# Index scores in groups of four, another order of attention units, sparse scaling on ScalarE, and low weights made by an adding transfer

## The chip, the cores and the metric

The kernel runs on one core of one Trainium2 chip. A core has five engines that run their own instruction queues in order and meet at semaphores: TensorE (PE, matrix products), VectorE (DVE), ScalarE (ACT), GpSimd (POOL) and SyncE (SP, which here only issues transfers). PE reads its operands from SBUF and writes to the eight banks of PSUM; DVE and ACT empty the banks. The metric is the device time of one execution in microseconds, as the median of several runs; lower is better.

## The reference, cut to what matters

Three transformer-like blocks follow each other on x, 512 tokens of 1024 features in float32. Block 1 is sparse attention with a gated unit and a convolved feed-forward; block 3 a state space and delta rule mixer. The change lies in block 2, which runs twice (l = 0, 1):

```python
h = rms_norm(x, g_mix[layer]);  proj = h @ w_in[layer]
qa, ka, va, iq, ik, iw, qb, kb, vb = split(proj)          # rope on qa, ka, iq, ik, qb, kb
dots = einsum('bqhd,bsd->bqhs', iq, ik) * IDX_DIM ** -0.5  # 8 index heads of 32
score = einsum('bqhs,bqh->bqs', relu(dots), iw * IDX_HEADS ** -0.5)
_, idx = top_k(where(admissible, score, -inf), 128)
out_a = softmax(qa . ka[idx]) . va[idx]                    # sparse attention, 8 heads of 64
out_b = differential attention of qb, kb, vb               # 4 heads, each the difference of two maps
x = x + concat([out_a, out_b]) @ w_out
x = x + (silu(h2 @ w_gate) * (h2 @ w_up)) @ w_down         # h2 = rms_norm(x, g_ffn)
```

## The kernel before

The stream x is held with features on the partitions, eight tiles of 128 x 512. A product in full precision is made of three passes of PE on operands split in two parts, high and low: high by high, high by low, low by high. The split of weights is made on the chip. `load_piece` (L278 to L285) lets SP fetch a piece of up to 128 x 1024 to a raw buffer (one of four), ACT makes the high part `whi` by a cast (L283), and DVE the low part `wlo` as raw less high (L284). `whi` and `wlo` each go round three buffers (`WS`), so a piece can be split as soon as PE has used up the third one before it. `lin_steps` (passes at L350 to L352) makes a block of 128 output features by 24 passes of 512 columns, and `tok_steps` (L333 to L335) does products with tokens on the partitions.

Block 2 begins with projections of the index queries and keys and their rotary embedding. `rope` copies a result (ACT, L871), lets four small transfers turn its halves (issued by ACT, L874), and forms the result with a product on POOL (L875), one on DVE (L876) and a sum on POOL (L877). After that come the index scores: for the query tiles qt = 1, 2, 3 (256, 384, 512 keys) and eight heads of 32 rows each, three passes into a bank of kind `s` (three banks), then a relu on ACT (L940) and an accumulation with the head's weight on DVE (L941). For each of the three tiles 16 calls of `top8` (L924, L925) find the 128 largest, one maximum of eight and one replacement each; they are queued in `top`, and a last step turns what is left into a mask. Then vB is projected (36 passes a token tile and half), and attention is mixed.

Attention has eight units, pairs of heads: 0 to 3 are differential, 4 to 7 sparse. A step is a unit and one of four query tiles. PLAN is the order of the 32 steps. In step j the scores of step j + 2 are formed (`scores` L354 to L374: six passes `s`, a masked reduction on DVE at L366, an exponential on ACT at L369), then `select` runs queued `top8` calls, then `turned` transposes the weights (L382, copied by ACT at L384), then the values are multiplied. Between them `feed` takes steps of `fill`: projections of the later units' queries and keys (`heads_steps`), of vA (`wtB`) and, when all of a layer's outputs of units 0 to 3 are there, the first half of the output product (`wout`, columns 512 on, in eight half pieces of 128 x 512). Before sparse weights are transposed, DVE scales them with the reciprocal of their row sum (L1027).

The order of instructions on each engine is made by a scheduler from the order of the program, its own costs and the buffers that come free; engines then run their queues in that order. So the diff alone does not tell what stands where in a queue.

Of the kernel before, what the change touches and what calls it, by code (L numbers as in the profile page):

```python
# [12 lines left out]
F32 = mybir.dt.float32  # L13
# [7 lines left out]
P = 128  # L21
# [9 lines left out]
# ---------------------------------------------------------------- host layout  # L31
def kpieces(w):
    """[K, M] -> [M/128, 128, K/128 * 128]: one block of columns per row, the contraction on partitions."""
    k, m = w.shape
    a = w.reshape(k // P, P, m // P, P).transpose(2, 1, 0, 3)
    return np.ascontiguousarray(a).reshape(m // P, P, k)


def kmajor(w):
    """[K, N] -> [128, K/128 * N]."""  # L40
    k, n = w.shape
    return np.ascontiguousarray(w.reshape(k // P, P, n).transpose(1, 0, 2)).reshape(P, -1)


def colvec(v):
    """[n * 128] -> [128, n]."""
    return np.ascontiguousarray(np.asarray(v).reshape(-1, P).T)
# [23 lines left out]
def prep(i):  # L71
# [22 lines left out]
    # block 1  # L94
# [43 lines left out]
    # block 2  # L138
# [31 lines left out]
    # block 3  # L170
# [27 lines left out]
# ---------------------------------------------------------------- device code  # L198
class Build:
    def __init__(self, tc, aps, offs, ctx):  # L200
        self.tc, self.nc, self.aps, self.offs = tc, tc.nc, aps, offs
        self.ctx = ctx
        self.uid = 0
        self.sb = ctx.enter_context(tc.tile_pool(name="sb", bufs=1))
# [15 lines left out]
    def t512(self, dt=F32, name="t"):  # L220
        """A [128, 512] slot, taken in program order and given back with free()."""
# [15 lines left out]
    def set_ring(self, **kinds):  # L237
        """Slots that short-lived tiles of a kind go round; 0 gives them back."""
# [13 lines left out]
    def banks(self, **kinds):  # L252
        """Which PSUM banks each kind of product goes round."""
# [22 lines left out]
    # weights: one DMA of [128, n <= 1024], then the exact two-part split  # L276
    def load_piece(self, ap):
        nc = self.nc  # L278
# [7 lines left out]

    def split(self, src, name="s", tiles=None):
        """src [128, n] F32 (SBUF or PSUM) -> hi, lo."""
# [6 lines left out]
    def lin_T(self, ap, xs, tag="mm", piece=None):  # L295
        """ap [128, K] (one block of 128 output rows); xs: list of (hi, lo) per k-tile -> PSUM [128, 512]."""
        return last_of(self.lin_steps(ap, xs, tag, piece))

    def lin_steps(self, ap, xs, tag="mm", piece=None):
        """lin_T, a k-tile a step; the last step gives the result."""  # L300
# [16 lines left out]
    def tok_steps(self, ap, n, xs, done, wide=1):  # L317
        """ap [128, 8 * n]: tokens on partitions, PSUM [128, n] per token tile to done(tt, ps)."""
# [22 lines left out]
    def scaled(self, o, scale, name):  # L341
        """o * scale in two parts."""
# [4 lines left out]
    def mm3(self, out, w, x, start=True, stop=True):  # L347
        """out (+)= w.T @ x, either operand in two parts."""
# [5 lines left out]
    def scores(self, q, k, qt, masks, mx, sm):  # L354
        """Per half: exp(max - (q.k + mask)) with its row sums; q carries the turned sign."""
# [19 lines left out]
    def turned(self, t, qt):  # L375
        """[queries, keys] -> the blocks of keys on partitions, [128, block, 128 queries]."""
# [10 lines left out]
    def rsqrt(self, y, v, pool=False):  # L387
        """y = v ** -0.5 on small [128, n] tiles; v is SBUF and positive."""
# [17 lines left out]
    def bcast_cols(self, col_of_tt, tag="at"):  # L406
        """[128 tokens, 128 (broadcast)] stationary per token tile -> PSUM [128, 512] rows."""
# [5 lines left out]
    def bcast_pairs(self, cols, tag="at"):  # L413
        """cols [128 tokens, 4, 2] -> PSUM [128 = (2, 64), 512]."""
# [4 lines left out]
    # sums of squares of the residual stream, and what follows from them  # L419
# [19 lines left out]
    def col_sums(self, *accs):  # L439
        """-> PSUM [128 tokens, 4]: sums over the partitions."""  # L440
# [9 lines left out]
    def stat_end(self, st):  # L450
        """-> [128 tokens, 4]: 1 / rms"""
# [13 lines left out]
    def norm_in(self, x, g, hi, lo):  # L465
        """hi + lo = x * g, g a per-partition column."""
# [6 lines left out]
    # ------------------------------------------------------------ block 1  # L473
    def block1(self, x, B, first, g_next, stats):
# [36 lines left out]
        # the overlapping windows of the compressed keys and values, position pairs on partitions  # L511
# [99 lines left out]
        # relative bias strips, sign turned: strip[p, h, c] = -bias[bucket(p + 384 - c)], masked where negative  # L611
# [30 lines left out]
        # the two halves of the spatial gating unit, in parts that go between others  # L642
# [28 lines left out]
        # q / k norms per head  # L671
# [16 lines left out]
        # compressed branch probabilities, transposed to [(r, n), q]  # L688
# [85 lines left out]
        # selected and windowed branches, head pair by head pair: scores ahead of transposes and values, with parts  # L774
        # of projections in between
# [63 lines left out]
        # convolved gated feed-forward, in two halves of its width  # L839
# [26 lines left out]
    # ------------------------------------------------------------ block 2  # L866
    def rope(self, ps, dim, cs, sn):
        """Rotary embedding of PSUM ps with the tables cs, sn."""
# [11 lines left out]
    def block2(self, l, x, xg, st, G, g_next, stats):  # L880
# [38 lines left out]
        # index scores and the 128 largest per query  # L919
# [7 lines left out]
        for qt in range(1, NT):  # L927
# [3 lines left out]
            for h in range(8):  # L931
                hs = slice(32 * (h % 4), 32 * (h % 4) + 32)
                ps = self.pst("s", "is")
                self.mm3(ps[:, :N], [p[hs, qt * P : N] for p in idx[1 + h // 4]], [p[hs, :N] for p in idx[0]])
                w = iw[:, qt, h : h + 1]
                if h == 0:
                    nc.vector.tensor_scalar(sc[:, :N], ps[:, :N], 0.0, w, op0=ALU.max, op1=ALU.mult)
                else:
# [35 lines left out]
        # A unit is a pair of heads (two maps of one, or two that share a block of rows), a step a unit's tile of  # L974
        # queries: scores two steps ahead, then transposes, then values, with parts of projections in between.
# [44 lines left out]
        # sparse attention over the selected keys  # L1020
# [95 lines left out]
        for _ in fill:  # L1116
            pass
# [628 lines left out]
```

## Time and profile before

| what | us |
|---|---|
| runs of the kernel | 3119.2, 3116.98, 3124.82 |
| median | 3119.2 |
| span of the profiled execution, first to last instruction | 3123.8 |
| block 2, layer 0 (index scores to first half of output), about | 711 to 1007 |
| block 2, layer 1 (the same), about | 1404 to 1700 |

Of the profiled execution the span is recorded, and no time of its own beside it; it lies within the range of the three runs. A row of windows gives each engine's busy time in a stretch, the number of instructions in parentheses, then the granted clock of PE as a share of full speed (1.00 is 2.4 GHz and 0.50 is 1.2 GHz), the share of time that DMA engines were busy, and what they moved. A row of a timeline gives start, length, engine, line, operation, what is written and read, shape and how many are drawn together; in brackets stands how long the engine had been idle before it and what released it. Busy time of DVE or ACT counts only where PE waits for it.

### The profile page before, as it was taken

Reading aid. Unit: us, or ns where it says so; the run is one execution under the profiler, and the core shown is the slowest. Engines: PE = TensorE matmul, PEld = TensorE weight load, DVE = VectorE, ACT = ScalarE, POOL = GpSimd, SP = SyncE. Lnnn points to the kernel's source line nnn. Section 1 sums busy time; section 2 is a strip of 40 time slices with the busy share of each in tenths; the row PEclk is TensorE's granted clock in tenths of the full one; section 3 lists DMA queues with packets and bytes.
Section 4 is the critical chain, followed back from the end, with each engine's and each line's share of the span. In section 5 each row is a group of like instructions: output and inputs, shape, how many; then the busy total and the mean of one; then the engine's idle time right before and its main releaser. Section 6 shows DMA issues by size and latency. Waiting matters only on the chain.

```text
span 3123.8 us, 40875 instructions
## 1 busy us (share of the span) xinstructions
PE 3052.9 (98%) x15416; PEld 2437.1 (78%) x15416; DVE 1785.8 (57%) x3400; ACT 1231.4 (39%) x2261; POOL 440.5 (14%) x411
## 2 busy tenths in 40 slices
PE   8999999999999999999999999999999999999998
PEld 6867888887677888887677888877777888888886
DVE  6576655647976333348866333369874665543333
ACT  4365433434455222234454222347543433322222
POOL 0001000011221101121211101110820000211011
PEclk9999999998999999998899999999999999999999
DMA  5402223332212223332213233236434222322322
GB/s 175 125 22 77 90 80 109 99 100 81 74 52 92 95 81 108 97 99 80 72 47 99 93 91 102 79 107 199 155 99 155 85 86 88 108 95 78 110 83 74
DMA packets 124052, 299.95 MB, mean 96 GB/s; under 512 B 28440, under 2 KB 40792, under 8 KB 123856
## 3 DMA queue, kind: packets, MB, share of 16 engines
q1 hardware_dynamic: 115696, 285.79, 29.2%
q10 hardware_dynamic: 7680, 9.97, 1.2%
q8 instruction: 122, 2.00, 0.3%
q0 software_dynamic: 480, 1.57, 0.1%
q14 instruction: 74, 0.61, 0.1%
HBM read 272.52 MB, written 14.79 MB: 92 GB/s over the span
## 4 chain that ended last, share of the span: by engine, by line
PE 87%; DVE 6%; DMA 2%; ACT 2%; POOL 1%; issue 1%; ACTq 1%; SPq 0%; DVEq 0%; POOLq 0%
PE p L350 24%; PE p L351 24%; PE p L352 24%; PE s L362 2%; DMA rope<-rope 2%; PE tr L382 1%; PE ss L444 1%; PE p L333 1%; ACTq L874 1%; DVE isc L925 1%; PE O L1036 1%; PE p L335 1%; PE p L334 1%; POOL rope L877 1%; DVE m L924 1%
## 5 line engine op out<-in xcount | busy, mean ns | idle before, releaser
L350 PE MATMUL p<-xh,whi 128*128 128x512 f32 x2360 | 955.4, 405 | 10.6 <-ACT xh L467 7.2
L283 ACT CAST whi<-wraw 128x1024 fp32r<-128x1024 f32 (+4 forms) x528 | 495.5, 940 | 1181.3 <-PE p L351 851.5
L351 PE MATMUL p<-xl,whi 128*128 128x512 f32 x2360 | 949.4, 402 | 0.5 <-DVE xl L468 0.5
L352 PE MATMUL p<-xh,wlo 128*128 128x512 f32 x2360 | 946.5, 401 | 1.1 <-DMA wraw<-in_b_cw1k 1.1
L284 DVE TENSOR_TENSOR wlo<-wraw,whi 128x1024 fp32r<-128x1024 f32 (+4 forms) x528 | 599.9, 1138 | 325.1 <-ACT whi L283 311.9
L350 PEld LDWEIGHTS p<-xh,whi 128*128 128x128 f32 x2360 | 448.4, 190 | 120.9 <-issue 8.8
L352 PEld LDWEIGHTS p<-xh,wlo 128*128 128x128 f32 x2360 | 447.5, 190 | 107.5 <-issue 4.8
L351 PEld LDWEIGHTS p<-xl,whi 128*128 128x128 f32 x2360 | 448.2, 190 | 103.1 <-issue 5.0
L350 PE MATMUL p<-acth,whi 128*128 128x512 f32 x704 | 277.8, 395 | 0.0
L352 PE MATMUL p<-acth,wlo 128*128 128x512 f32 x704 | 277.7, 394 | 0.0
L351 PE MATMUL p<-actl,whi 128*128 128x512 f32 x704 | 277.5, 394 | 0.0
L1612 POOL TENSOR_TENSOR g<-g,rbc 128x512 f32<-128x512 f32 x66 | 114.0, 1728 | 808.5 <-ACT g L1611 808.5
L436 POOL TENSOR_TENSOR sqacc<-sqacc,sq 128x512 f32<-128x512 f32 x63 | 97.4, 1550 | 777.0 <-ACT sq L434 776.8
L1614 DVE TENSOR_TENSOR g<-g,p 128x512 f32<-128x512 f32 x66 | 45.4, 688 | 238.7 <-PE p L352 238.7
L352 PEld LDWEIGHTS p<-acth,wlo 128*128 128x128 f32 x704 | 132.2, 188 | 31.6
L351 PEld LDWEIGHTS p<-actl,whi 128*128 128x128 f32 x704 | 132.2, 188 | 31.5
L350 PEld LDWEIGHTS p<-acth,whi 128*128 128x128 f32 x704 | 132.2, 188 | 31.3
L1610 DVE TENSOR_TENSOR g<-p,rbc 128x512 f32<-128x512 f32 x66 | 45.7, 692 | 188.1 <-PE p L352 188.1
L369 ACT ACTIVATE stile<-stile,sm 128x128 f32<-128x128 f32 (+3 forms) x192 | 106.8, 557 | 83.3 <-DVE sm L366 72.1
L1634 DVE TENSOR_TENSOR x<-x,p 128x512 f32<-128x512 f32 x96 | 66.0, 688 | 108.1 <-PE p L352 107.9
L333 PE MATMUL p<-whi,xh 128*128 128x256 f32 (+2 forms) x352 | 104.6, 298 | 0.3 <-ACT rope L871 0.3
L334 PE MATMUL p<-wlo,xh 128*128 128x256 f32 (+2 forms) x352 | 102.9, 293 | 0.0
(457 smaller groups left out, 4183.4 us busy)
## 6 DMA issues: line engine op xcount, KB each, us to landing
wraw<-in_b_wup SPq DMA_DIRECT2D x176, 512.0 KB, 3.3
wraw<-in_b_win SPq DMA_DIRECT2D x118, 512.0 KB, 3.6
wraw<-in_b_wdn SPq DMA_DIRECT2D x64, 512.0 KB, 3.5
wraw<-in_b_wout SPq DMA_DIRECT2D x48, 256.0 KB, 2.7
wraw<-in_b_wdn SPq DMA_DIRECT2D x64, 192.0 KB, 2.3
rope<-rope ACTq DMA_DIRECT2D x128, 64.0 KB, 2.3
row<-rows SPq DMA_DIRECT2D x32, 256.0 KB, 4.4
wraw<-in_b_wtC SPq DMA_DIRECT2D x8, 512.0 KB, 4.0
```

Source lines behind the costliest of these rows:

```text
L283: nc.scalar.copy(hi, raw)
L284: nc.vector.tensor_tensor(lo, raw, hi.bitcast(F32), op=ALU.subtract)
L333: mm(ps, xs[k][0][:, ts], wh[:, s], start=k == 0, stop=False)
L334: mm(ps, xs[k][0][:, ts], wl[:, s], start=False, stop=False)
L350: mm(out, w[0], x[0], start=start, stop=False)
L351: mm(out, w[0], x[1], start=False, stop=False)
L352: mm(out, w[1], x[0], start=False, stop=stop)
L362: self.nc.tensor.matmul(out[g][:, :n], q[i][hs, qt * P : n], k[j][hs, :n], start=c == 0, stop=c == 2)
L369: nc.scalar.activation(t[:, :n], t[:, :n], AF.Exp, bias=mx[:, g : g + 1], scale=-1.0, accum_out=sm[:, g : g + 1])
L436: eng.tensor_tensor(accs[i], accs[i], sq, op=ALU.add)
L1612: nc.gpsimd.tensor_tensor(g, g, rbc, op=ALU.mult)
L1634: nc.vector.tensor_tensor(x[m], x[m], ps, op=ALU.add)
```

## The change

Four edits, all in block 2. First, index scores are formed for four heads at a time: of each of the three passes the four heads (on the four quarters of PE's rows) follow each other, and the kind `s` has four banks (2 to 5) instead of three, `mm` three instead of four, in this stage. Second, PLAN places all steps of units 0 to 3 ahead of those of unit 4, and `select` runs three calls a step in place of four. Third, the scaling of sparse weights moves from DVE to ACT. Fourth, from the first step of mixing to the end of the first half of the output product, pieces of weights are split by `load_piece_rmw`: ACT makes high by a copy and low = -high by a second one, and POOL issues a transfer that reads the same weights from memory and adds them to low. These are 24 pieces a layer: 14 of heads, 2 of `wtB`, 8 half pieces of `wout`.

```diff
+    def load_piece_rmw(self, ap):
+        nc = self.nc
+        n = ap.shape[1]
+        raw = self.t([P, 1024], tag="wraw", bufs=self.WR, name="wraw")[:, :n]
+        nc.sync.dma_start(raw, ap)
+        hi, lo = (self.t([P, 1024], tag=tg, bufs=self.WS, dt=F32R, name=tg)[:, :n] for tg in ("whi", "wlo"))
+        nc.scalar.copy(hi, raw)
+        nc.scalar.activation(lo, hi.bitcast(F32), AF.Copy, scale=-1.0)
+        nc.gpsimd.dma_start(lo, ap, accum_op=ALU.add)
+        return hi, lo
...
+        self.banks(mm=(0, 1, 6), s=(2, 3, 4, 5), at=(7,))
+        quarter = [slice(32 * r, 32 * r + 32) for r in range(4)]
...
-            for h in range(8):
-                hs = slice(32 * (h % 4), 32 * (h % 4) + 32)
-                ps = self.pst("s", "is")
-                self.mm3(ps[:, :N], [p[hs, qt * P : N] for p in idx[1 + h // 4]], [p[hs, :N] for p in idx[0]])
+            for hg in range(2):
+                pss = [self.pst("s", "is") for _ in range(4)]
+                for c, (i, j) in enumerate(((0, 0), (0, 1), (1, 0))):
+                    for ps, hs in zip(pss, quarter):
+                        nc.tensor.matmul(
+                            ps[:, :N], idx[1 + hg][i][hs, qt * P : N], idx[0][j][hs, :N], start=c == 0, stop=c == 2
+                        )
...
-                nc.vector.tensor_scalar(tb[g][:, :N], tb[g][:, :N], f[:, g : g + 1], None, op0=ALU.mult)
+                nc.scalar.activation(tb[g][:, :N], tb[g][:, :N], AF.Copy, scale=f[:, g : g + 1])
...
         fill = filling()
         fed = [0]
+        self.rmw = True
...
-            select(4 * (j + 1))
+            select(3 * (j + 1))
...
         for _ in fill:
             pass
+        self.rmw = False
...
-PLAN = "00 01 02 03 10 11 12 13 20 40 21 22 41 42 23 30 31 32 33 43 50 51 52 53 60 61 62 63 70 71 72 73"
+PLAN = "00 01 02 03 10 11 12 13 20 21 22 23 30 31 32 33 40 41 42 43 50 51 52 53 60 61 62 63 70 71 72 73"
```

In the queues this gives the following, for layer 0. On PE, the first three heads of the last query tile's index scores (`is`, one number a head; `idxh` and `idxl` are the parts of index queries and keys) before:

```order
L350 MATMUL is_6587<-idxh_6151,idxh_6200 128x512
L351 MATMUL is_6587<-idxl_6152,idxh_6200 128x512
L352 MATMUL is_6587<-idxh_6151,idxl_6201 128x512
L350 MATMUL is_6592<-idxh_6151,idxh_6200 128x512
L351 MATMUL is_6592<-idxl_6152,idxh_6200 128x512
L352 MATMUL is_6592<-idxh_6151,idxl_6201 128x512
L350 MATMUL is_6599<-idxh_6151,idxh_6200 128x512
L351 MATMUL is_6599<-idxl_6152,idxh_6200 128x512
L352 MATMUL is_6599<-idxh_6151,idxl_6201 128x512
```

and after, where the lines have moved with the text:

```order
L952 MATMUL is_6587<-idxh_6151,idxh_6200 128x512
L952 MATMUL is_6587<-idxl_6152,idxh_6200 128x512
L952 MATMUL is_6588<-idxh_6151,idxh_6200 128x512
L952 MATMUL is_6588<-idxl_6152,idxh_6200 128x512
L952 MATMUL is_6589<-idxh_6151,idxh_6200 128x512
L952 MATMUL is_6589<-idxl_6152,idxh_6200 128x512
L952 MATMUL is_6587<-idxh_6151,idxl_6201 128x512
L952 MATMUL is_6588<-idxh_6151,idxl_6201 128x512
L952 MATMUL is_6589<-idxh_6151,idxl_6201 128x512
```

The passes of a head no longer stand next to each other; the heads alternate, by threes at this place, and the fourth follows alone. Of the tile before this one, the first head of each group of four has moved up among the passes of vB: the first stood behind 36 of these and stands behind 2, the fifth behind 15, the other six behind 27 and more.

On DVE, what precedes the first reduction of attention scores (`stile` from `s`) in layer 0, before (`isc` are the index scores of a tile, `m` the eight largest):

```order
L924 MAX m_1528_7194<-isc_6474 128x8
L925 MATCH_REPLACE isc_6474<-m_1528_7194,isc_6474 128x256
L924 MAX m_1529_7197<-isc_6474 128x8
L925 MATCH_REPLACE isc_6474<-m_1529_7197,isc_6474 128x256
L924 MAX m_1530_7200<-isc_6474 128x8
L924 MAX m_1553_7292<-isc_6530 128x8
L925 MATCH_REPLACE isc_6474<-m_1530_7200,isc_6474 128x256
L925 MATCH_REPLACE isc_6530<-m_1553_7292,isc_6530 128x384
L284 TENSOR_TENSOR wlo_7019<-wraw_7016,whi_7018 128x1024
L1084 TENSOR_SCALAR isc_6474<-isc_6474 128x256
L366 ISA stile_6903,sm_6892<-s_6895,b_cmask_6060 128x128
L366 ISA sm_6892 128x1
```

and after:

```order
L942 MATCH_REPLACE isc_6474<-m_1565_7344,isc_6474 128x256
L942 MATCH_REPLACE isc_6530<-m_1566_7348,isc_6530 128x384
L1106 TENSOR_SCALAR isc_6474<-isc_6474 128x256
L941 MAX m_1587_7417<-isc_6530 128x8
L942 MATCH_REPLACE isc_6530<-m_1587_7417,isc_6530 128x384
L941 MAX m_1588_7420<-isc_6530 128x8
L942 MATCH_REPLACE isc_6530<-m_1588_7420,isc_6530 128x384
L941 MAX m_1589_7423<-isc_6530 128x8
L381 ISA stile_6903,sm_6892<-s_6895,b_cmask_6060 128x128
L381 ISA sm_6892 128x1
L381 ISA stile_6906,sm_6892<-s_6896,b_cmask_6060 128x128
L381 ISA sm_6892 128x1
```

The splits `wlo` are gone from this place, and more of the second tile's search stands ahead of the first reduction.

On POOL, the stretch before that holds the rope operations of the later units:

```order
L875 TENSOR_TENSOR rope_8092<-rope_8092,tab_6100 128x512
L877 TENSOR_TENSOR rope_8092<-rope_8092,rope_8093 128x512
L875 TENSOR_TENSOR rope_8454<-rope_8454,tab_6100 128x512
L877 TENSOR_TENSOR rope_8454<-rope_8454,rope_8455 128x512
L875 TENSOR_TENSOR rope_8540<-rope_8540,tab_6100 128x512
L877 TENSOR_TENSOR rope_8540<-rope_8540,rope_8541 128x512
L875 TENSOR_TENSOR rope_8657<-rope_8657,tab_6100 128x512
L877 TENSOR_TENSOR rope_8657<-rope_8657,rope_8658 128x512
L875 TENSOR_TENSOR rope_8770<-rope_8770,tab_6100 128x512
L877 TENSOR_TENSOR rope_8770<-rope_8770,rope_8771 128x512
```

and after, from the same unit on, with the issues of the adding transfers for vA, heads and the first half pieces of the output between them:

```order
L890 TENSOR_TENSOR rope_7869<-rope_7869,tab_6100 128x512
L892 TENSOR_TENSOR rope_7869<-rope_7869,rope_7870 128x512
L890 TENSOR_TENSOR rope_7966<-rope_7966,tab_6100 128x512
L892 TENSOR_TENSOR rope_7966<-rope_7966,rope_7967 128x512
L299 DMA wlo_8108<-in_b_wtB 128x1024
L299 DMA wlo_8127<-in_b_wtB 128x1024
L890 TENSOR_TENSOR rope_8090<-rope_8090,tab_6100 128x512
L892 TENSOR_TENSOR rope_8090<-rope_8090,rope_8091 128x512
L299 DMA wlo_8362<-in_b_win 128x1024
L299 DMA wlo_8488<-in_b_win 128x1024
L299 DMA wlo_8591<-in_b_win 128x1024
L890 TENSOR_TENSOR rope_8467<-rope_8467,tab_6100 128x512
```

Each `DMA` row is an issue that POOL makes when ACT has written the negated high part; what follows it in the queue comes after it.

## Rows read from the trace of the kernel before

**Rows 1.** The page: busy time, share of the span, instructions of each engine.
```profile
PE 3052.9 (98%) x15416; PEld 2437.1 (78%) x15416; DVE 1785.8 (57%) x3400; ACT 1231.4 (39%) x2261; POOL 440.5 (14%) x411
```

**Rows 2.** Windows of busy time in us; the last is of layer 1.
```profile
711.00:740.00 29.00, 24.80 (x129) 19.14 (x124) 18.03 (x21) 12.77 (x25) 9.87 (x7) 0.83 0.38 112
740.00:772.00 32.00, 30.04 (x194) 26.29 (x193) 27.41 (x73) 14.43 (x25) 0.29 (x2) 0.78 0.12 37
772.00:845.00 73.00, 66.26 (x310) 50.17 (x310) 68.67 (x189) 31.66 (x86) 20.14 (x21) 0.92 0.30 91
845.00:975.00 130.00, 126.92 (x760) 93.09 (x758) 90.71 (x255) 70.10 (x184) 23.60 (x23) 1.00 0.17 50
1465.00:1538.00 73.00, 65.80 (x309) 49.93 (x310) 69.95 (x191) 31.67 (x86) 20.88 (x22) 0.91 0.31 90
```

**Rows 3.** Waits of PE, 740 to 980: total us, times, longest.
```profile
PE s L362 <- ACT kh L291: 6.6, 4, 2.9
...
PE s L362 <- DVE sm L366: 1.7, 1, 1.7
```

**Rows 4.** Waits of PE in layer 1, 1434 to 1669.
```profile
PE s L362 <- ACT kh L291: 8.6, 4, 3.3
```

**Rows 5.** Timeline of PE, index scores: start, length, instruction, [idle before].
```profile
745.02 0.82 PE L350 MATMUL is<-idxh,idxh 32*128 32x512 f32 x3
745.61 0.65 PE L351 MATMUL is<-idxl,idxh 32*128 32x512 f32 x3
746.04 0.65 PE L352 MATMUL is<-idxh,idxl 32*128 32x512 f32 x3
747.35 1.28 PE L350 MATMUL is<-idxh,idxh 32*128 32x512 f32 x2 [0.66 <-ACT relu L940]
```

**Rows 6.** Groups by form, 733 to 751: count, busy us, mean ns, idle.
```profile
L941 DVE SCALAR_TENSOR_TENSOR isc<-relu,iw,isc 128x512 f32<-128x512 f32 x6 | 4.4, 741 | 0.8 <-ACT relu L940 0.8
...
L940 ACT ACTIVATE relu<-is 128x512 f32<-128x512 f32 x7 | 3.9, 597 | 3.6 <-PE is L352 3.6
```

**Rows 7.** Timeline of all engines, the rope chain of one k.
```profile
791.78 2.44 ACTq L874 DMA_DIRECT2D rope<-rope  x4
...
796.66 1.28 POOL L875 TENSOR_TENSOR rope<-rope,tab 128x512 f32<-128x512 f32 x1 [6.05 <-DMA rope<-rope]
...
798.65 2.11 POOL L877 TENSOR_TENSOR rope<-rope,rope 128x512 f32<-128x512 f32 x1 [0.71 <-DVE rope L876]
...
800.80 0.62 ACT L291 CAST kh<-rope 128x512 fp32r<-128x512 f32 x1 [3.12 <-POOL rope L877]
...
801.47 0.49 PE L362 MATMUL s<-kh,qh 64*128 64x128 f32 x3 [2.13 <-ACT kh L291]
```

**Rows 8.** Window of the ten microseconds around that wait.
```profile
800.00:810.00 10.00, 8.53 (x31) 5.91 (x31) 8.30 (x29) 3.81 (x14) 3.83 (x6) 0.66 0.24 74
```

**Rows 9.** Groups by form, 757 to 850.
```profile
L284 DVE TENSOR_TENSOR wlo<-wraw,whi 128x1024 fp32r<-128x1024 f32 x11 | 13.9, 1274 | 0.0
...
L283 ACT CAST whi<-wraw 128x1024 fp32r<-128x1024 f32 x12 | 12.5, 1044 | 7.0 <-PE p L351 6.1 <-PE p L335 0.9
...
L924 DVE MAX8 m<-isc 128x8 f32<-128x384 f32 x16 | 8.9, 556 | 0.2
L925 DVE MATCH_REPLACE8 isc<-m,isc 128x384 f32<-128x384 f32 x16 | 8.7, 543 | 0.0
```

**Rows 10.** Line L1027, both layers: ns min/median/max, first and last start.
```profile
L1027 DVE TENSOR_SCALAR stile<-stile,sm x64: 275/413/1418, 845.7 to 1657.8; 128x128 f32<-128x128 f32 x16, 128x256 f32<-128x256 f32 x16, 128x384 f32<-128x384 f32 x16, 128x512 f32<-128x512 f32 x16
```

**Rows 11.** DMA issues, 686 to 1007: count, KB each, us to landing.
```profile
wraw<-in_b_win SPq DMA_DIRECT2D x15, 512.0 KB, 3.8
...
wraw<-in_b_wout SPq DMA_DIRECT2D x16, 256.0 KB, 2.7
```

**Rows 12.** DMA issues by POOL in block 3, 2190 to 2262.
```profile
sys<-dAT POOLq DMA_DIRECT2D x2, 256.0 KB, 6.4
dT<-sys POOLq DMA_DIRECT2D x2, 256.0 KB, 3.7
```

More of the change, by code (lines that the diff above doesn't have):

```diff
@@ L277, in load_piece @@
     def load_piece(self, ap):
+        if self.rmw:
+            return self.load_piece_rmw(ap)
         nc = self.nc
@@ L930, in block2 @@
             msl.append(sc)
-            for h in range(8):
-                hs = slice(32 * (h % 4), 32 * (h % 4) + 32)
-                ps = self.pst("s", "is")
-                self.mm3(ps[:, :N], [p[hs, qt * P : N] for p in idx[1 + h // 4]], [p[hs, :N] for p in idx[0]])
[L935 to L938, printed above, removed]
+            for hg in range(2):
[5 more added lines that the diff above has]
+                        )
+                for h, ps in enumerate(pss, 4 * hg):
+                    w = iw[:, qt, h : h + 1]
+                    if h == 0:
+                        nc.vector.tensor_scalar(sc[:, :N], ps[:, :N], 0.0, w, op0=ALU.max, op1=ALU.mult)
+                        continue
                     r = self.tmp(name="relu")
@@ L1117, in block2 @@
             pass
+        self.rmw = False
         self.free(vA, msl, cmask, mix[4:])
```

## The prediction

> **What bounds the kernel now.** I read the page first. TensorE (PE) is busy for 98% of the span and no other engine for more than 57% [rows 1], so time can be gained only where PE stands still or runs at the lower of its two clock levels (1.2 GHz, 0.5 in the clock column; 2.4 GHz is 1.00). I then cut layer 0 of block 2 into stages by windows of busy time [rows 2]. What a stage lost is its length less PE's busy time weighted with the clock: 29 - 24.80 x 0.83 = 8.4 us in 711 to 740 (index projections, first index scores), 32 - 30.04 x 0.78 = 8.6 us in 740 to 772 (last index scores, projection of vB, first attention scores), 73 - 66.26 x 0.92 = 12.0 us in 772 to 845 (mixing of units 0 to 4 with the search for the 128 largest), and 130 - 126.92 = 3.1 us in 845 to 975. The same stage of layer 1 shows 73 - 65.80 x 0.91 = 13.1 us. That is about 32 us a layer: 64 us, 2%, is the ceiling for everything that the change can give. Even the part it can touch does not all belong to it.
>
> The waits say which engine PE stood waiting for in 740 to 980 [rows 3]: k's high part, which ACT makes, 6.6 us in four waits, against 1.7 us for DVE's score reduction. In layer 1 the wait for k is 8.6 us [rows 4]. DVE is 94% busy in 772 to 845 (68.67 of 73) and ACT 43% [rows 2], so DVE is crowded there, and yet PE's waits name it once. It stands behind the others: in the chain up to the wait at 801.47 [rows 7] the rope DMAs are issued at 791.78, POOL begins its product at 796.66, its sum at 798.65, and ACT's cast at 800.80 releases PE after 2.13 us idle. Of the ten microseconds, the DMAs have almost five and POOL's two products 3.4; DVE stands between them with one operation (from 797.94, where POOL's product ends, to 798.65: 0.7 us). The clock then falls: 0.66 in 800 to 810 [rows 8], which costs 10 - 8.53 x 0.66 = 4.4 us where the idle was 2.1. A wait of about 2 us therefore costs about twice itself.
>
> **Index scores by fours.** A matmul pass 512 wide takes 0.43 us at the lower level (745.61 to 746.04), so 0.215 at the higher. Nine matmuls of three heads that begin at 745.02 have all run when PE falls idle 0.66 us before 747.35, at 746.69 [rows 5]: 1.67 us where nine one behind another would take 9 x 0.43 = 3.9. So heads on different quarters of the rows already run beside each other; the new order does not create that. The row after them says what PE waits for: ACT's relu, so the emptying of banks. The Trainium skill, "TensorEngine Tiling (Array Packing)", section "Theoretical Speedup", gives up to four times for a contraction of 32 tiled by rows; by that, the 27.6 thousand columns of a layer's scores, 11.6 us one behind another, would fall to 2.9 and the change would gain 8 us a layer. By the rows here most of that is had already.
>
> That emptying is DVE's and ACT's: one relu 512 wide takes 597 ns on ACT and one accumulation 741 ns on DVE [rows 6], and neither changes in count. What changes is that four banks instead of three take scores, and that the first heads of the next-to-last tile move up among the passes of vB (the first stood behind 36 of these and now stands behind 2, the fifth behind 15; the other six behind 27 and more), so that 14 heads in place of 16 are left to be emptied in one run, at about 0.74 us each. The losses to be had are the 8.4 and 8.6 us of the first two stages; the last scores still end on DVE's chain. Two heads less and a bank more are 3 x 0.74 = 2.2 us, and the lower clock that such a wait brings, half as much again: I take 3.5 us a layer, between -2 (mm has one bank fewer) and 9 (the stage's whole loss).
>
> **Differential heads first, 3 selections a step.** DVE's search for one tile is spread over more steps: 16 passes at 3 a step instead of 4. A maximum over 384 columns costs 556 ns and its replacement 543 [rows 9], so one selection less per step frees 1.1 us of DVE in a step of about 6 us (32 steps between 772 and 975). The first unit's DVE wait (1.7 us) and some of the fall of the clock behind it can go, but by the order DVE does three and a half passes of the second tile ahead of the first scores, where it had done one pass and two splits (one is in the rows shown, the other 20 rows ahead): 2.5 x 1.1 us more against 2 x 1.27 less, so nothing at that very place. Bounds -2 to 4 us a layer; I take 1.5.
>
> **Sparse scaling on ScalarE.** 32 scalings a layer of 413 ns leave DVE [rows 10], 13 us, and arrive on ACT at about the relu's 597 ns for 512 wide, so about 14 us in all. ACT has 60 us free in 845 to 975 (70.10 of 130) and PE lost 3.1 us there: worth between -2 and 1 us, I take 0.
>
> **Low weights made by a transfer that adds.** 24 pieces a layer: 14 of 512 KB for heads, 2 for vA, 8 of 256 KB for the output. DVE loses 16 x 1.27 + 8 x 0.6 = 25 us a layer [rows 9]; in 757 to 850 that is 13.9 of its 93 us, in which it was nearly full. ACT gets a negated copy for each, priced by the cast beside it at 1.04 us [rows 9]: 16 x 1.04 + 8 x 0.52 = 21 us, of which 12 us fall in 757 to 850, where ACT has room. DVE's relief shortens every chain that passes it (rope, score reduction): of the 12.0 us lost in 772 to 845 I give it a third, 4 us, between 0 and 9; the greater part of the rope chain is DMA and POOL and stays.
>
> The price is a longer way to the low part. Now it is cast and subtraction, 1.04 + 1.27 = 2.3 us [rows 9]. After, it is cast, negated copy, an issue on POOL and a transfer, which must also come after whatever stands ahead of it in POOL's queue. No transfer that adds is in this trace. From the rows [rows 11, 12]: a plain 512 KB from SyncE lands in 3.8 us, 256 KB in 2.7; POOL's own 256 KB land in 3.7 to 6.4. So the low end is 3.8 us for 512 KB and 2.7 for 256, and the high end is twice POOL's worst for 512 KB, 12.8, and 6.4 for 256. I take 5.5 and 4, near POOL's lower rows (its 6.4 was measured in a busy stretch). The way is then 1.04 + 1.04 + 0.6 + 5.5 = 8.2 us for a whole piece and 0.52 + 0.52 + 0.6 + 4 = 5.6 us for a half (0.6 us for the issue is an estimate from ACT's four rope issues in 2.44 us [rows 7]).
>
> What covers it: the ring has three low buffers, so a piece may start when the third before it is used up, with two pieces of PE's work ahead of it. A whole piece is 24 passes x 0.215 = 5.2 us, two are 10.3 us, and attention lies between them: 8.2 is covered. The two vA pieces are used in one tile of tokens together, with only 12 short passes between them, and POOL puts a rope pair ahead of them; I count 2 us of waiting. A half piece is 12 passes, 2.6 us; two are 5.2 us against 5.6: 0.4 us for most of the first halves, where little attention lies between, plus POOL's rope in the queue (1.3 us): 2 us. One of the two waits brings the lower clock, 3 us. Together -7 us a layer. At the low end this is -1, at the high end each of 14 pieces comes (15.5 - 10.3) = 5 us late, less what attention covers, some -30 us a layer.
>
> The Trainium skill, "SBUF — State Buffer", section "SBUF: two separate sides", warns that a transfer issued by POOL starves for descriptors while DVE runs an operation in its two-port mode, such as a float32 copy; this speaks against the change, and by it the first rival below would come true wherever DVE is in that mode. Whether the landings of 3.7 to 6.4 us [rows 12] hold such a delay the rows do not tell.
>
> **Sum.** 3.5 + 1.5 + 0 + 4 - 7 = 2 us a layer, and 2 us a layer for the clock that one wait taken away gives back (half of 4.4, as at 801): 4 us, for two layers 8 us. The profiled execution has a span of 3123.8 us, 4.6 over the median of the runs, 3119.2, and inside their spread (3117.0 to 3124.8); nothing that lies around it is touched, so I take the difference from the median: 3111 us. A measurement of this kernel can tell about 0.3%, 9.4 us, from no change, so the forecast lies at that bound.
>
> **Rivals.**
> - The adding transfer is late everywhere. If the landing is over 8 us for 512 KB, the way (1.04 + 1.04 + 0.6 + 8) passes 10.3 us and PE waits for the low part at about half of the pieces; 5 waits of 2 us a layer, doubled by the clock as at 801, are 20 us against gains of 11: +9 a layer, 3119 + 18 = 3137 us, the time I give this case; with 8 waits 3119 + 42 = 3161. For it speaks that POOL's rows for half the size reach 6.4 us and that POOL's queue also holds the rope chain's two links, which a waiting issue blocks. Against it, that DMA engines are only 17 to 31% busy here [rows 2]. From three late pieces a layer on (12 us against 11) it decides the sign. Chance 0.27.
> - Nothing to be had: PE's waits are the rope chain's (DMA and POOL), DVE and ACT were covered. Then gains of 5 us at the index scores and losses of 5 a layer leave 3119 us. For it, rows 3 and 7. Chance 0.22.
> - The crowded DVE was behind nearly all of it. Then 9 of the 12.0 and 13.1 us in the mixing stage and 8 of the first two come back, with 2 us of waiting: 15 a layer, 3119 - 30 = 3089 us. For it, DVE's 94%; against it, one DVE wait in rows 3. Chance 0.21.
> - My own case, 3103 to 3117 us: 0.30.
>
> Faster by over 0.3% (below 3109.8) takes the third case, half of mine and a little of the second and first: 0.21 + 0.15 + 0.06 = 0.42. Slower (above 3128.6) takes most of the first and a little of the second: 0.28. Within 0.3%: 0.30. The range leaves out the ends of the first and third: 3082 to 3146. My own case spans 3103 to 3117.
>
> **What would show it.** Right: the rows of 740 to 772 show a clock above 0.85; DVE below 85% in 772 to 845; waits of PE for k at most as long as before; waits named "wlo" or the adding transfer only at vA and the first output halves, below 5 us a layer. Wrong: landings of the adding transfer above 8 us, or POOL standing on it while rope is queued; or unchanged waits for k with DVE half empty, which says that DVE never mattered.

## The result, and the profile after

The changed kernel takes 3156.2 us (median of 4 runs, 3150.4 to 3160.4) against 3120.6 for the kernel before (4 runs): ratio 1.0100, interval 1.0081 to 1.0119. It is slower by 1%, outside the range forecast and on the side that the first rival had. The profiled execution took 3157.2 us with a span of 3155.4, 31.6 over the span before.

The page: busy time, the granted clock in 40 slices, and the queue of POOL's transfers.

```profile
PE 3063.4 (97%) x15416; PEld 2444.9 (77%) x15416; DVE 1720.0 (55%) x3288; ACT 1295.7 (41%) x2373; POOL 476.1 (15%) x459
...
PEclk8999999998899999998899999999999999999999
...
q0 software_dynamic: 7392, 22.55, 4.0%
```

DVE lost 66 us of work against [rows 1] and ACT gained 64; POOL's queue moves 22.6 MB. PE's busy time grew by 10.5 us for the same work, which is time at the lower clock, and it stood idle 21 us longer. The same stages as in [rows 2] (length, then PE, PEld, DVE, ACT, POOL busy, clock, DMA share, GB/s; the last is layer 1, shifted by as much as layer 0 had lost):

```profile
711.00:740.00 29.00, 25.10 (x137) 19.36 (x136) 18.32 (x25) 13.07 (x26) 8.51 (x6) 0.88 0.39 115
740.00:772.00 32.00, 28.26 (x196) 25.30 (x195) 29.14 (x79) 16.31 (x26) 3.69 (x5) 0.84 0.24 70
772.00:845.00 73.00, 66.45 (x277) 48.53 (x277) 59.69 (x178) 35.62 (x92) 21.57 (x27) 0.81 0.49 112
845.00:975.00 130.00, 117.61 (x698) 87.58 (x697) 60.96 (x191) 85.50 (x210) 36.89 (x37) 0.99 0.42 97
1480.00:1553.00 73.00, 67.86 (x289) 49.41 (x289) 62.28 (x186) 36.88 (x95) 21.27 (x29) 0.84 0.50 114
```

Counted as in the forecast, length less PE's busy time by the clock, the four stages of layer 0 lose 29 - 25.10 x 0.88 = 6.9, 32 - 28.26 x 0.84 = 8.3, 73 - 66.45 x 0.81 = 19.2 and 130 - 117.61 x 0.99 = 13.6 us, together 48.0, where before they lost 32.1. That is 16 us a layer, and twice that is the difference of the spans. All of it is in the mixing of attention (7.2 and 10.5 us more); the two stages ahead gave back 1.8 us. The row of layer 1 loses 73 - 67.86 x 0.84 = 16.0 us against 13.1. DVE fell to 82% in 772 to 845 as forecast, and PE lost more.

PE's waits in layer 0, 680 to 1020 (total us, times, longest):

```profile
PE s L377 <- ACT kh L306: 6.9, 5, 2.5
PE p L349 <- DMA wlo<-in_b_wtB: 2.9, 2, 1.8
PE p L367 <- DMA wlo<-in_b_wout: 2.5, 2, 1.3
PE is L952 <- ACT vA L927: 2.5, 1, 2.5
PE s L377 <- DVE sm L381: 2.2, 1, 2.2
PE is L952 <- ACT relu L961: 2.1, 1, 2.1
PE O L1017 <- ACT pts L399: 2.0, 2, 1.1
PE p L367 <- DMA wlo<-in_b_win: 1.6, 1, 1.6
```

Seven us are waits for the adding transfer itself (2.9 + 2.5 + 1.6). The wait for k is 6.9 us over this stretch against 6.6 in [rows 3], though DVE has been relieved. The transfers (count, KB, us from issue to landing), to be held against [rows 11, 12]:

```profile
wraw<-in_b_win SPq DMA_DIRECT2D x15, 512.0 KB, 3.8
wlo<-in_b_win POOLq DMA_DIRECT2D x14, 512.0 KB, 5.4
...
wlo<-in_b_wout POOLq DMA_DIRECT2D x8, 256.0 KB, 4.9
...
wlo<-in_b_wtB POOLq DMA_DIRECT2D x2, 512.0 KB, 5.5
```

And one half piece of the output in the timeline (start, length, instruction, idle before it):

```profile
948.31 0.60 ACT L384 ACTIVATE stile<-stile,sm 128x384 f32<-128x384 f32 x1
...
949.05 0.63 ACT L298 ACTIVATE wlo<-whi 128x512 fp32r<-128x512 f32 x1
...
949.98 0.88 POOL L299 DMA_DIRECT2D wlo<-in_b_wout  x1 [3.49 <-ACT wlo L298]
...
954.12 0.50 PE L367 MATMUL p<-oh,wlo 128*128 128x512 f32 x1 [1.31 <-DMA wlo<-in_b_wout]
```

ACT's exponentials stand ahead of the negated copy, POOL has idled 3.49 us for it, issues at 949.98, and PE, 1.31 us idle, gets the low part at 954.12. The way of the low part begins in ACT's queue, and 5.1 us from copy to use are what the prediction had counted without that queue.

### The profile page after: what moved, and what is told of

Read it like the earlier page. It is cut to its first block, busy times and chain, and to the rows that moved or that the text cites. A ratio compares the mean times of both kernels' runs of the same rounds, so it can differ in the third digit from the quotient of the medians.

```text
span 3155.4 us, 40937 instructions
## 1 busy us (share of the span) xinstructions
PE 3063.4 (97%) x15416; PEld 2444.9 (77%) x15416; DVE 1720.0 (55%) x3288; ACT 1295.7 (41%) x2373; POOL 476.1 (15%) x459
## 4 chain that ended last, share of the span: by engine, by line
PE 83%; DVE 6%; DMA 3%; ACT 3%; issue 2%; POOL 1%; ACTq 1%; SPq 0%; DVEq 0%; POOLq 0%
PE p L365 23%; PE p L367 23%; PE p L366 23%; PE s L377 2%; DMA rope<-rope 2%; PE tr L397 1%; PE ss L459 1%; DVE isc L942 1%; PE p L348 1%; PE p L350 1%; PE p L349 1%; ACTq L889 1%; DVE m L941 1%; PE O L1057 1%; PE O L822 1%
## 5 line engine op out<-in xcount | busy, mean ns | idle before, releaser
L286 ACT CAST whi<-wraw 128x1024 fp32r<-128x1024 f32 (+3 forms) x480 | 452.4, 943 | 1159.4 <-PE p L366 825.4
L287 DVE TENSOR_TENSOR wlo<-wraw,whi 128x1024 fp32r<-128x1024 f32 (+3 forms) x480 | 542.8, 1131 | 314.4 <-ACT whi L286 304.5
L365 PEld LDWEIGHTS p<-acth,whi 128*128 128x128 f32 x704 | 132.2, 188 | 31.6
L384 ACT ACTIVATE stile<-stile,sm 128x128 f32<-128x128 f32 (+1 forms) x192 | 106.3, 555 | 51.9 <-DVE sm L381 45.7
```

Of the source, the lines that this page charges most:

```text
L286: nc.scalar.copy(hi, raw)
L287: nc.vector.tensor_tensor(lo, raw, hi.bitcast(F32), op=ALU.subtract)
L365: mm(out, w[0], x[0], start=start, stop=False)
L384: nc.scalar.activation(t[:, :n], t[:, :n], AF.Exp, bias=mx[:, g : g + 1], scale=-1.0, accum_out=sm[:, g : g + 1])
```

## Experiments

All times are medians; a ratio is to runs of the kernel before on the same chip. Where nothing else is said the edit is made to the changed kernel.

**The four edits apart.** Without the adding transfer (`e1_no_add`):

```diff
-        self.rmw = True
```

> The changed kernel with DVE's split kept for all pieces (no adding transfer); the other three edits stay. Theory A (the adding transfer costs the time: PE's waits for the low part, POOL's queue, ACT's second copy): all of the 36 us and a little more come back, 3105 to 3122 us. Theory B (the new order of the steps and 3 selections costs it, because what hid the work of sparse steps is used up earlier): 3140 to 3156 us. Theory C (index scores by fours cost it): 3140 to 3156 us too; the next runs tell B from C.

Measured 3124.2 us, ratio 1.0006 (0.9994 to 1.0017): 2 us above theory A's range, but level with the kernel before, which took 3124.3 us beside it. The kernel before with the adding transfer alone (`e2_add_only`):

```diff
+        self.rmw = True   # and load_piece_rmw
```

> The kernel before with the adding transfer alone (order of steps, 4 selections, index scores and DVE's scaling as before). Theory A: 3145 to 3165 us, with waits of PE for the low part of 5 to 8 us a layer and DVE under 85% busy in the mixing stage. Theories B and C: 3105 to 3125 us.

Measured 3157.1 us, ratio 1.0101 (1.0081 to 1.0120). Each way round, the adding transfer is the whole of the loss: theory A, and the other three edits together are worth nothing that can be told.

Of what theory A expected of `e2_add_only`, though, only the time came. PE waits for the low part 2.4 us in layer 0 and 4.8 in layer 1, not 5 to 8, and DVE is busy 67.22 of the 73 us in 772 to 845, 92% and not under 85%. The waits for k fell, to 3.4 us in layer 0 and 3.9 in layer 1 from 6.6 and 8.6 [rows 3, 4]. What grew is PE's busy time, by 27.4 us against [rows 1], of the 36.2 us by which the span is longer. Its page, two windows, and its waits for k and the low part in 680 to 1020:

```profile
PE 3080.3 (97%) x15416; PEld 2453.8 (78%) x15416; DVE 1737.6 (55%) x3352; ACT 1270.0 (40%) x2309; POOL 477.1 (15%) x459
```

```profile
845.00:975.00 130.00, 123.66 (x663) 89.46 (x662) 61.65 (x209) 72.42 (x182) 36.20 (x37) 0.87 0.41 89
850.00:870.00 20.00, 20.00 (x55) 11.80 (x55) 9.11 (x33) 9.59 (x27) 3.70 (x5) 0.53 0.29 69
```

```profile
PE s L377 <- ACT kh L306: 3.4, 3, 1.7
...
PE p L349 <- DMA wlo<-in_b_wtB: 2.2, 2, 2.0
...
PE p L367 <- DMA wlo<-in_b_win: 0.2, 1, 0.2
```

In 845 to 975 the clock is 0.87 where it was 1.00 before. Ahead of 850 PE had idled 1.08 us for k's high part and 0.79 us for its low part; then it was busy for all of 850 to 870, at 0.53. So a loss of the same size is here mostly time at the lower clock, at this place behind short waits for other things than the low part, and PE's waits for the low part do not measure it. Why the clock falls more often than before is not shown.

The kernel before with the order of steps alone (`e3_plan_only`):

```diff
-            select(4 * (j + 1))
+            select(3 * (j + 1))   # and the new PLAN
```

> The kernel before with the order of steps of the changed kernel and 3 selections a step alone. Theory A: 3112 to 3124 us (my term for this was a gain of 1.5 us a layer). Theory B: 3140 to 3156 us.

Measured 3122.4 us, ratio 0.9994 (0.9981 to 1.0007): nothing. The kernel before with the fours alone (`e4_fours_only`):

```diff
-                self.mm3(ps[:, :N], ...)   # head by head
+                for c, (i, j) in enumerate(((0, 0), (0, 1), (1, 0))):   # four heads a pass, four banks
```

> The kernel before with index scores by fours and their banks alone. Theory A: 3110 to 3120 us (my term for this was a gain of 3.5 us a layer). Theory C: 3140 to 3156 us.

Measured 3134.8 us, ratio 1.0029 (1.0009 to 1.0049), between the theories, with runs from 3114 to 3140. Its profiled execution has lost 1 us up to the start of layer 1's mixing at 1445; in layer 1's mixing, which the edit does not touch, the clock was lower, by these windows:

```profile
1540.00:1600.00 60.00, 58.41 (x328) 44.28 (x328) 46.34 (x136) 32.40 (x93) 11.88 (x15) 0.87 0.13 39
1600.00:1660.00 60.00, 57.74 (x316) 40.71 (x316) 33.37 (x94) 27.64 (x70) 11.29 (x8) 0.91 0.17 51
```

In the kernel before the same two windows show 0.98 and 1.00. Whether the edit causes that is open. The order and the scaling on ACT without fours and without the transfer (`g3_plan_and_scale`):

```diff
-                nc.vector.tensor_scalar(tb[g][:, :N], ...)
+                nc.scalar.activation(tb[g][:, :N], tb[g][:, :N], AF.Copy, scale=f[:, g : g + 1])   # beside the new PLAN
```

> The kernel before with the order of steps, 3 selections and the scaling on ACT, without the fours and without the adding transfer. The fours alone cost 0.3%, the order alone nothing; if these add up: 3112 to 3122 us, the best of all so far. If the scaling loads ACT where it matters: 3125 to 3135 us.

Measured 3122.2 us, ratio 0.9996 (0.9984 to 1.0008). Within its interval it is the kernel before; no version here beats that.

**What in the adding transfer costs.** ACT's copies without any transfer (`h2_copy_then_split`), where DVE overwrites the copy with its split:

```diff
-        nc.gpsimd.dma_start(lo, ap, accum_op=ALU.add)
+        nc.vector.tensor_tensor(lo, raw, hi.bitcast(F32), op=ALU.subtract)
```

> The changed kernel with ACT's negated copy into the low part, which DVE then overwrites with its split; no transfer by POOL, and all slots: ACT's load alone, without the dead buffer. If the copies on ACT cost 16 us: 3135 to 3146 us. If the run with the dead buffer was slow for its order or slots: 3120 to 3130 us.

Measured 3136.9 us, ratio 1.0047 (1.0034 to 1.0059), clear of e1. Busy time in 757 to 1010 of e1 and of this run (columns as in [rows 2]):

```profile
757.00:1010.00 253.00, 241.19 (x1338) 183.04 (x1337) 182.29 (x484) 139.15 (x339) 50.86 (x50) 0.95 0.24 73
```

```profile
757.00:1010.00 253.00, 239.95 (x1280) 178.85 (x1279) 178.66 (x467) 153.00 (x355) 51.89 (x50) 0.95 0.22 70
```

ACT's load goes from 55% to 60%. The two profiled executions took 3132.7 and 3133.1 us, so these windows show the load and not the loss, which stands in the ratios. PE's waits in the same stretch of e1, then of this run:

```profile
PE s L377 <- ACT kh L306: 4.9, 3, 4.0
...
PE O L1017 <- ACT pts L399: 0.3, 1, 0.3
```

```profile
PE s L377 <- ACT kh L306: 6.1, 3, 2.4
...
PE O L1057 <- ACT pts L399: 1.4, 1, 1.4
PE O L1017 <- ACT pts L399: 1.1, 3, 0.5
```

The waits for what ACT makes, k and the transposed weights, rise from 5.2 to 8.6 us, while those for DVE fall. DVE's split also comes after ACT's copy here, which may cost something of its own; the copies into a buffer of their own, below, do not have that. A plain transfer in place of the adding one (`f1_plain_transfer`; the low part then holds the raw weight):

```diff
-        nc.gpsimd.dma_start(lo, ap, accum_op=ALU.add)
+        nc.gpsimd.dma_start(lo, ap)
```

> The changed kernel, where POOL's transfer of the 48 pieces does not add but only writes (the low part then holds the raw weight, so the output is not the reference's); the copies on ACT and all queues stay. Theory A1 (adding itself is slow: the transfer reads both sides): landings fall from 5.4 us to under 4.2 and the time to 3125 to 3138 us. Theory A2 (the way over ACT, POOL's queue and a transfer is too long whatever the transfer does): landings of 4.5 to 5.4 us, 3145 to 3158 us.

Measured 3142.2 us, ratio 1.0061 (1.0047 to 1.0075). Its landings:

```profile
wlo<-in_b_win POOLq DMA_DIRECT2D x14, 512.0 KB, 4.1
...
wlo<-in_b_wout POOLq DMA_DIRECT2D x8, 256.0 KB, 3.4
...
wlo<-in_b_wtB POOLq DMA_DIRECT2D x2, 512.0 KB, 3.9
```

A plain transfer of POOL lands 1.3 to 1.6 us sooner than the adding one. The time lies a little above theory A1's and clear of the changed kernel's: adding itself costs some 0.4% of the 1.0%. PE's waits for the low part are 3.3 us in 757 to 1010 (1.9 + 0.9 + 0.5) against 7.0. Against h2, which has the copies and no transfer, the interval overlaps: with a plain transfer the way over POOL costs nothing that can be told beyond the copies. The adding transfer for heads alone (`f2_heads_only`):

```diff
-        self.rmw = True   # for all fill pieces
+                self.rmw = True   # around the load of a head's piece only
```

> The changed kernel with the adding transfer for the 28 pieces of heads alone; the 4 pieces of vA and the 16 half pieces of the output are split by DVE again. Theory A3 (PE's waits at vA and at the first output halves are most of the loss, as the prediction's term of 7 us a layer had it): 3124 to 3136 us. Theory A4 (the loss lies in the mixing of the heads, by ACT's second copies and POOL's queue in the chain of k): 3140 to 3156 us.

Measured 3142.9 us, ratio 1.0060 (1.0046 to 1.0075). The 4 pieces of vA and the 16 halves make about 0.4% of the 1.0%, the 28 pieces of heads the rest over e1. The time lies in A4's range, but A3's places have a part of the loss too.

**Runs with a dead buffer.** These let PE read DVE's split and do the rest of the work for nothing, into a buffer that nobody reads. To make room for it the pool has two slots (tiles of 128 x 512) fewer. Their control (`g1_two_slots_fewer`), the copies (`f3_copy_only`), and copies and transfers (`f4_unwaited`):

```diff
-NS = 66
+NS = 64
```

> The changed kernel with DVE's split for all pieces and two slots of the pool fewer, nothing else: the control for the two runs with a dead buffer. If ACT's second copy was what cost in those: 3118 to 3128 us, as without the adding transfer. If the missing slots did: 3138 to 3150 us.

```diff
+        nc.scalar.activation(dead, hi.bitcast(F32), AF.Copy, scale=-1.0)
```

> The changed kernel with DVE's split for all pieces, no adding transfer, and ACT's negated copy of 48 pieces written to a dead buffer (two slots fewer to make room): ACT has the work of the change, and PE waits for nothing new. Theory A4, ACT's part: 3138 to 3156 us. If ACT has room: 3118 to 3130 us.

```diff
+        nc.scalar.activation(dead, hi.bitcast(F32), AF.Copy, scale=-1.0)
+        nc.gpsimd.dma_start(dead, ap, accum_op=ALU.add)
```

> As the run before, and POOL also issues the adding transfers, into the dead buffer: all of the change's work on ACT, POOL and the DMA queues is done, but PE reads the low part that DVE makes and waits for none of it. If PE's wait for the low part is the cause: 3118 to 3132 us. If POOL's queue and the DMA traffic are (rope's links stand behind issues): 3140 to 3160 us, with more waiting for k.

Measured 3129.2 us (1.0015, 1.0003 to 1.0028), 3145.2 (1.0073, 1.0060 to 1.0085) and 3152.5 (1.0091, 1.0075 to 1.0106). The copies cost 0.6% over the control, a little more than in the run without the buffer (0.4%). PE's waits for what ACT makes in 757 to 1010, of the control, then of the copies:

```profile
PE s L377 <- ACT kh L306: 4.8, 3, 4.0
...
PE O L1017 <- ACT pts L399: 0.4, 1, 0.4
```

```profile
PE s L378 <- ACT kh L307: 7.0, 4, 2.4
PE O L1058 <- ACT pts L400: 3.5, 2, 1.9
PE O L1018 <- ACT pts L400: 2.1, 1, 2.1
```

They rise from 5.2 to 12.6 us, with the clock at 0.95 in both. f4's interval touches f3's and the changed kernel's, so the transfers beside the copies and PE's wait for the low part are not parted here. Nor is f4 clean: it has one dead buffer, and ACT's next copy into it stood 8 times, 15.2 us over both layers, for the landing of the transfer before. In f4 the 64 KB rope transfers land later than in e1; in the changed kernel, which is as slow, they do not. e1's first, then f4's, then the changed kernel's:

```profile
rope<-rope ACTq DMA_DIRECT2D x56, 64.0 KB, 2.0
```

```profile
dead<-in_b_win POOLq DMA_DIRECT2D x14, 512.0 KB, 5.5
...
rope<-rope ACTq DMA_DIRECT2D x56, 64.0 KB, 3.3
```

```profile
rope<-rope ACTq DMA_DIRECT2D x56, 64.0 KB, 2.1
```

In `e2_add_only` they take 2.1 us too, so the late landing is no part of what the change costs.

Two runs were to show POOL's queue and the DMA traffic without ACT's copies, `g4_transfers_only` and `h1_transfers_in_place`:

```diff
+        nc.gpsimd.dma_start(self.dead[:, :n], ap, accum_op=ALU.add)   # g4
```

> The changed kernel with DVE's split for all pieces and two slots fewer, and POOL's 48 adding transfers into a dead buffer that is cleared once a layer, with no copies on ACT: POOL's queue and the DMA traffic alone. If they cost little by themselves (the run before with copies and transfers was 7 us over that with copies): 3120 to 3132 us. If they cost as the copies do: 3138 to 3150 us.

```diff
+        nc.scalar.copy(dead[:, :1], hi.bitcast(F32)[:, :1])   # h1: one column
+        nc.gpsimd.dma_start(dead, ap, accum_op=ALU.add)
```

> As the run with copies and unwaited transfers (3152 us), but ACT's negated copy of a piece shrinks to one column, which only holds the transfer to its place in time: POOL's queue and the DMA traffic in the mixing stage, without ACT's load. Control with two slots fewer: 3129 us. If the three costs add (copies 16, queue and traffic 7, waits of PE 9): 3132 to 3140 us, and rope's transfers land in 3.3 us in place of 2.0. If ACT's copies are nothing by themselves: 3146 to 3155 us.

Measured 3187.6 us (1.0205, 1.0185 to 1.0226) and 3173.6 (1.0167, 1.0153 to 1.0181), beyond all that was expected, and neither answers its question. In g4 nothing held the transfers to their place: they ran from 4.4 us on, in block 1, each standing on POOL for the landing of the one before.

```profile
L299 POOL DMA_DIRECT2D dead<-in_b_win x28: 846/855/1039, 4.4 to 251.1; - x28
```

In h1 ACT itself stood 11 times for a landing, since there is one dead buffer, as in f4 (layer 0):

```profile
ACT dead L300 <- DMA dead<-in_b_win: 9.2, 6, 3.0
...
ACT dead L300 <- DMA dead<-in_b_wout: 8.5, 5, 2.8
```

Both show engines standing in order for transfers, POOL in g4 and ACT in h1, beside losses of 2.1 and 1.7%; what share of that loss the standing has, neither separates. Last, the negated copy on DVE (`g2_copy_on_dve`):

```diff
-        nc.scalar.activation(lo, hi.bitcast(F32), AF.Copy, scale=-1.0)
+        nc.vector.tensor_scalar(lo, hi.bitcast(F32), -1.0, None, op0=ALU.mult)
```

> The changed kernel with the negated copy made by DVE instead of ACT; the adding transfer and its wait stay. If ACT's second copies (1.05 us each, between its copies of weights and of k) cost most: 3125 to 3140 us. If the longer way and POOL's queue cost most: 3148 to 3165 us.

Measured 3179.0 us, ratio 1.0180 (1.0159 to 1.0200), beyond both. PE's wait for k, and POOL's waits at its issues, layer 0:

```profile
PE s L377 <- ACT kh L306: 14.2, 5, 3.5
```

```profile
POOL wlo L299 <- DVE wlo L298: 51.9, 9, 12.4
```

DVE's copy (686 ns in the middle) stands behind the search for the 128 largest; POOL stands at an issue up to 12.4 us for it, and the wait for k doubles. That rope's links stood behind those issues fits the order, but no run separates it from the rope transfers' later landing (3.5 us in the middle against 2.0 in e1).

## Why the prediction was wrong

- The term that failed is the price of the longer way to the low part, 7 us a layer. With DVE's relief of 4 the whole edit was forecast to lose 3; measured are 16 (1.0101 alone, 3157.1 less 3124.3 us, for two layers). The landing was sized right for whole pieces (5.5 taken, 5.4 measured) and too low for halves (4 taken, 4.9 measured).
- What the term left out is ACT: "where ACT has room" counted 21 us of copies at nothing, since ACT was 43% busy. h2 shows them to cost 0.4% (1.0047 against 1.0006), some 6 us a layer, and f3 0.6% over its control, some 9. The share of busy time said nothing of it: k's cast, the transposed weights and the copies stand in that one queue, and in f3 PE's waits for the first two rise by 7.4 us in layer 0. The rest is adding itself, 0.4% (f1), some 6 us a layer, part of it in waits for the low part.
- The waits at vA and the first halves were forecast in their places, 2 + 2 us a layer; the profile has 2.9 + 2.5, and a head piece that was called covered has 1.6. With the clock behind them and their own copies f2 puts vA and halves at 0.4%, some 6 us a layer, where the prediction had 2 + 2 + 3: this part had about the right size, though by luck in part, since the copies in it were counted at nothing. In e2 the waits came smaller (2.2 us at vA, none at the halves of layer 0) and the loss was as large, so the waits themselves are not the whole mechanism. That the pieces of heads cost nothing was not: f2 still loses 0.5% over e1, and the copies of these pieces, 28 of 40 whole ones' worth, can explain a little over half of that by h2.
- DVE's relief, 4 us a layer, is not seen as time. DVE fell to 82%, below the mark that was set, and PE's wait for k stayed (6.6 to 6.9 us), which fits the second rival: the wait was the rope chain's, DMA, POOL and ACT, and not DVE's. It is not proof. The same edit loaded ACT and POOL, and in e2 the wait for k did fall by half; no run relieves DVE of these splits without loading another engine.
- Index scores, 3.5 us a layer: nothing or a loss (e4; e1 against g3 is 1.0006 against 0.9996). The rows said that heads already ran side by side, and that held; the term stood on the added bank and on two heads fewer to empty, and neither showed as a gain. (In the estimate set beside it, 11.6 less 2.9 is 8.7, not 8; nothing rests on it.) Before, PE waited in this stage seven times a layer for ACT's relu or DVE's accumulation, 3.8 us in layer 0 and 3.5 in layer 1; after, in layer 0, two long waits make most of 5 us:

```profile
715.33 0.58 PE L952 MATMUL is<-idxh,idxh 32*128 32x256 f32 x1 [2.49 <-ACT vA L927]
...
742.62 1.17 PE L952 MATMUL is<-idxh,idxh 32*128 32x512 f32 x2 [2.05 <-ACT relu L961]
```

  The first is for ACT's emptying of vA's product, at the fourth head: the bank added to the scores had belonged to the projections (2.49 us). The second is for a relu (2.05).
- Order and 3 selections, 1.5 us a layer, and the clock's 2 us: not seen (e3, 0.9994). The scaling on ACT at 0 was right (g3).
- The first rival had the sign, and the mechanism by half: late low parts, on PE's path. Its condition, landings over 8 us for 512 KB, did not come (5.4), and its time, 3137 us, had the copies for nothing as well.

The Trainium skill's warning of POOL's transfers beside DVE, "SBUF — State Buffer", section "SBUF: two separate sides", does not show in the issues: in g2, where DVE makes a float32 copy with the factor -1 for each piece, POOL's issue takes 874 ns in the middle against 871 in the changed kernel. The landing of whole pieces of heads is 6.4 us there against 5.4, which may hold some of it; in which mode DVE ran no run shows.

What stays open: how the part beyond the copies divides between PE's waits for the low part, POOL's queue and the DMA traffic, and why the clock takes most of the loss in e2; the three runs with unwaited transfers (f4, g4, h1) stood on their own buffer.

## What to carry to other kernels

Before work is moved from a crowded engine to one that is half idle, ask what PE waits for from the receiving engine: here more copies on ACT, 43% busy, cost 0.4 to 0.6%, and no gain was seen from relieving DVE, 94% busy. Price a replaced step by its whole way, every queue that it passes in order included, and measure that way against the work between a buffer's release and its first use. Where the bottleneck engine waits rarely, a few waits of 1 to 2 us a layer and the clock behind them make up a change of 1%; so read the clock beside the waits. Give a buffer that serves only an experiment as many turns as the one it stands for, or the run measures the buffer.

## What the runs showed of the hardware

- An adding transfer of 512 KB into SBUF lands in 5.4 us in the middle (changed kernel; 6.4 in g2), a plain one by POOL in 4.1 (f1), SyncE's plain one in 3.8; of 256 KB in 4.9 (4.0 in f4), 3.4 and 2.7. An issue on POOL takes 0.87 us, not the 0.6 taken from ACT's.
- Moving 107 GB/s with adding transfers kept the DMA engines busy 45% of 757 to 1010 (changed kernel); 109 GB/s with plain ones 36% (f1).
- Beside adding transfers rope's 64 KB landed in 2.1 us in the middle in the changed kernel and in e2, in 3.3 in f4 and 3.5 in g2, against 2.0 without them (e1). What delays them in the last two is not shown.
- After two waits of 1.08 and 0.79 us PE was busy for all of 850 to 870 in e2, at a granted clock of 0.53.
